# Earlier row transposes and another order of copies, scalings and key doubling in the attention of a decoder trunk

## The chip, the cores and the metric

The kernel runs on one core of a Trainium2 chip. The metric is device time in microseconds (us) of one launch. The engines are named as the profile names them: PE multiplies matrices (PEld loads its weights), DVE and ACT work on vectors and read what PE leaves in PSUM, POOL and SP issue most DMAs. Each engine works through its own queue in order, and an instruction waits at its head until what it needs is there.

## The reference

One decoder layer on 512 tokens of width 1024, in float32: two attentions side by side, merged by gates, then an MLP with a short convolution.

```python
h = _rmsnorm(x, norm1_g[l]) * (1.0 + scale1) + shift1
proj = h @ w_in[l]
qa, ka, va, qd, kd, vd, ga, gd = jnp.split(proj, points, axis=-1)
out_a = _sliding_window_attention(...)   # 8 heads, 2 key heads, window 128, sinks
out_d = _diff_attention(...)             # 4 heads, two softmax maps each, below
merged = (jax.nn.sigmoid(ga) * (out_a @ w_branch_swa[l])
          + jax.nn.sigmoid(gd) * (out_d @ w_branch_diff[l]))
x = x + gate1 * (merged @ w_out[l])
h2 = _rmsnorm(x, norm2_g[l]) * (1.0 + scale2) + shift2
x = x + gate2 * _conv_ffn(h2, ...)       # then a final rmsnorm

# inside _diff_attention, for a block of 128 queries:
p = jax.nn.softmax(scores, axis=-1)
a = p[:, :, 0] - lam * p[:, :, 1]
out = einsum('bhqs,bshe->bqhe', a, v)
# and over all blocks: each head's 128 values are normed
out = _rmsnorm(out, subln_g) * (1.0 - lam_init)
```

## The kernel before

Float32 precision is had from a faster product: every operand is split into a high part (a cast, on ACT) and a low part (the difference, on DVE), and three products high x high, high x low, low x high are summed (lines 123 to 125). So each weight tile costs PE, ACT and DVE work.

The work runs in stages: the first projections (to about 57 us of the span), the two attentions with the remaining projections between their steps (to about 250 us), the output projection, the MLP. This case is about the attentions.

**Queues.** PE's order in attention is written out by hand. `fill(n)` puts n *ticks* of projection work (three products of one 128-row piece) between the steps of attention; `after(n, fn)` calls `fn` n ticks later. DVE and ACT are ordered by a scheduler: `tc.high_priority(offset=HP)` ranks what is inside ahead of other ready work (a larger offset ranks higher), `tc.issue_after` sets a lower bound.

**Names.** `stack` (L433) makes scaled queries in two copies, one with high and low parts on swapped halves of the partitions: ACT scales the high part (L438), DVE makes the low part (L441). `qa` are the queries of the windowed attention, in four pairs of heads; pair 1 is made from `aqa1` (`acc[2]`). `qk` holds a head's queries and keys of the differential attention; `double` (L445) makes its keys: casts on ACT (L448), low parts on DVE (L450), then two copies across halves (L452), one on DVE and one on ACT. Windowed pairs: `sw` scores, `st` and `lsum` softmax, `tp` transposes on PE, `pT` their copies on ACT (L619), `oa` values. Differential heads 0 to 3, each with four query blocks n: `sd` scores (PE L675), L686 bias and minimum on DVE, L701 exponentials on ACT, L704 to L706 on DVE, `td` transposes, `aTh`/`aTl` their parts. `ta` (L787 on ACT) empties a gate's projection `pga` from one of two banks tagged "f".

**A head's norm.** `diff_values(h)` multiplies probabilities and values into `od`. ACT makes `sq` (squares) and `of` (scaled values). Six ticks later (`STAT_LAG`) PE sums the squares (`pss`, L739), DVE and POOL form the inverse root as four columns (L154 to L166). `ROW_LAG` ticks after that `to_rows` turns the columns into a row: a transpose on PE (L102), a copy on ACT (`rs0p` to `rs3p`, L105), and two DMAs on POOL's queue (L107, L108), out to DRAM and back to all partitions as `rb`. `NORM_LAG` ticks after the sums `spread` multiplies `of` by `rb` (DVE L752) and splits the product into `vvh` (ACT) and `vvl` (DVE), both by `split` (L120). `od`, `pss` and the turned row share one bank tagged "v". `ada_rows` puts 32 unrelated row sums (`ra`, L776) on DVE; `wga`, `wba`, `wgd`, `wbd` are weight tiles split on ACT and DVE; `pB` is the last product of attention that needs `vvh` and `vvl`.

Of the kernel before, what the change touches and what calls it, by code (L numbers as in the profile page):

```python
# [27 lines left out]
HP = 100000  # L28
# [2 lines left out]
ADA_EVERY = 5  # L31
G1_AT = 12
M5_AT = 4
STAT_LAG = 6
ROW_LAG = (16, 16, 16, 10)
NORM_LAG = (30, 30, 30, 24)
VA_AT = 5
SWA_FILL = (2, 1, 6, 2, 2, 2, 2, 5, 0)
# [9 lines left out]
def kernel(  # L48
# [19 lines left out]
    nc = tc.nc  # L68
# [16 lines left out]
    def fbank(name):  # L85
        return bank("f", 2, [P, S], name)

    def sbank(name, shape=(P, S)):
        return bank("s", 3, list(shape), name)
# [29 lines left out]
    def split(hi, lo, src):  # L119
        return nc.scalar.copy(hi, src), nc.vector.tensor_sub(lo, src, hi.bitcast(F32))  # L120
# [104 lines left out]
    acc = [sbank("aka"), sbank("aqa0"), sbank("aqa1"), fbank("av0"), fbank("av1"), vbank("ava"), tbank("av2"), tbank("av3")]  # L225
# [10 lines left out]
    qsc = cpool.tile([P, 4], F32, name="qsc")  # L236
# [180 lines left out]
    qa = big.tile([P, 4, 2, S], F32R, tag="qa", name="qa")  # L417
# [12 lines left out]

    halves = ((lower, upper), (upper, lower))

    def stack(dst, src, scale, soon=True, high=True, low=True):  # L433
        with tc.high_priority(offset=HP) if soon else ExitStack():
            sc = [scale if isinstance(scale, float) else scale[own] for own, _ in halves]
            for j in range(2) if high else ():
                own = halves[j][0]
                nc.scalar.activation(dst[own, j], src[own], AF.Copy, scale=sc[j])  # L438
            for j in range(2) if low else ():
                own, other = halves[j]  # L440
                nc.vector.scalar_tensor_tensor(  # L441
                    dst[other, j], src[own], sc[j], dst[own, j].bitcast(F32), ALU.mult, ALU.subtract
                )

    def double(dst, src):  # L445
        with tc.high_priority(offset=HP):
            for j, (own, _) in enumerate(halves):
                nc.scalar.copy(dst[own, j, 0], src[own])  # L448
            for j, (own, _) in enumerate(halves):
                nc.vector.tensor_sub(dst[own, j, 1], src[own], dst[own, j, 0].bitcast(F32))  # L450
            for j, (own, other) in enumerate(halves):
                (nc.vector.tensor_copy, nc.scalar.copy)[j](dst[other, j], dst[own, j])  # L452

    vv = [big.tile([P, DIFF_HEADS, S], F32R, tag=f"vv{g}", name=f"vv{g}") for g in "hl"]
    vaT = big.tile([P, S], F32, tag="sq2", name="vaT")

    def keep_v(i, parts=(0, 1)):
        t = TOKENS[i] * P
        hi, lo = (v[:, :, t : t + P] for v in vv)
        src = acc[i].rearrange("p (h d) -> p h d", d=P)  # L460
        if 0 in parts:
            nc.scalar.copy(hi, src)
        if 1 in parts:
            nc.vector.tensor_sub(lo, src, hi.bitcast(F32))
# [23 lines left out]
    nc.vector.scalar_tensor_tensor(  # L488
        qa[lower, 0, 1], acc[1][upper], qsc[upper, 0:1], qa[upper, 0, 1].bitcast(F32), ALU.mult, ALU.subtract
    )  # L490
    stack(qa[:, 1], acc[2], qsc[:, 1:2], soon=False, low=False)
    keep_v(6, (0,))
    vat_copy = nc.scalar.copy(vaT, acc[5])
    man.close()
# [51 lines left out]
    def after(n, fn):  # L546
        later.append([n, fn])
# [42 lines left out]
    def swa_softmax(i):  # L590
        with tc.high_priority(offset=HP):
            c = pairs[i]
            for j in range(2):
                h = i + 4 * j
                nc.scalar.activation(c.es[:, j], c.nm[:, j], AF.Exp, bias=sink[:, h : h + 1])
                for n in range(NT):
                    w = P if n == 0 else 2 * P
                    nc.scalar.activation(
                        c.sb[n][:, j, :w], c.sb[n][:, j, :w], AF.Exp, bias=c.nm[:, j, n : n + 1], scale=-1.0,
                        accum_out=c.lsum[:, j, n : n + 1],  # L600
                    )
                nc.vector.tensor_add(c.lsum[:, j], c.lsum[:, j], c.es[:, j])
                nc.vector.reciprocal(c.lsum[:, j], c.lsum[:, j])
                for n in range(NT):
                    w = P if n == 0 else 2 * P
                    c.end = nc.vector.tensor_scalar_mul(c.sb[n][:, j, :w], c.sb[n][:, j, :w], c.lsum[:, j, n : n + 1])

    def swa_transpose(i, j):
        c = pairs[i]
        pt = ap.tile([P, 1024], F32, tag=("aTh", "aTl")[j], bufs=2, name=f"pT{i}_{j}")  # L610
        for b in range(2):
            wb = 512 if b == 0 else 384
            tp = tbank(f"tp{i}_{j}_{b}")
            for m in range(wb // P):
                kb, n = 2 * b + m // 2, 2 * b + m // 2 + m % 2
                off = (kb - max(0, n - 1)) * P
                nc.tensor.transpose(tp[:, m * P : (m + 1) * P], c.sb[n][:, j, off : off + P], ident)
            with tc.high_priority(offset=HP):
                c.copy = nc.scalar.copy(pt[:, b * 512 : b * 512 + wb], tp[:, :wb])  # L619
        c.pT.append(pt)  # L620

# [23 lines left out]
    def add_head(h):  # L645
        def q(wts):
            t = heads[h] = ap.tile([P, 6, S], F32R, tag="qk", bufs=2, name=f"qk{h}")
            o = fbank(f"pq{h}")
            yield from steps(o, wts, hT, KT)
            stack(t[:, 0:2], o, 2.0 ** (2 * h - 1))  # L650

        def k(wts):
            t = heads[h]
            o = fbank(f"pk{h}")
            yield from steps(o, wts, hT, KT)
            double(t[:, 2:6].rearrange("p (j b) s -> p j b s", b=2), o)

        for run, n in ((q, TILE_QD), (k, TILE_KD)):
            units.append((lambda n=n: load_tile(n + h, f"w{n}_{h}"), run))
# [61 lines left out]
    def diff_values(h):  # L721
        aTh, aTl = aTs[h]
        o = vbank(f"od{h}")
        for k in range(NT):
            q0 = k * P
            mm3(
                o[:, q0:], vv[0][:, h, k * P : (k + 1) * P], vv[1][:, h, k * P : (k + 1) * P],
                aTh[:, k * AW + q0 : k * AW + 512], aTl[:, k * AW + q0 : k * AW + 512],
                k == 0, k == NT - 1,
            )  # L730
        sq = big.tile([P, S], F32, tag="sq2", name=f"sq{h}")
        of = big.tile([P, S], F32, tag=("kvA", "kvB")[h % 2], name=f"of{h}")
        nc.scalar.activation(sq, o, AF.Square)
        nc.scalar.activation(of, o, AF.Copy, scale=sublnc)

        def stats():
            pss = vbank(f"pss{h}", (P, NT))
            for n in range(NT):
                nc.tensor.matmul(pss[:, n : n + 1], sq[:, n * P : (n + 1) * P], ones[:, 0:1], start=True, stop=True)  # L739
            rs = cols[:, NCOL + NT * h : NCOL + NT * h + NT]  # L740
            l0, e0 = sums[h][:, 0], sums[h][:, 1]
            nc.vector.scalar_tensor_tensor(e0, l0, EPS, l0, ALU.mult, ALU.mult)
            with tc.high_priority(offset=HP):
                rstd_m2(rs, pss, NT, P, ap, plus=e0)
            last = h == DIFF_HEADS - 1
            rb = big.tile([P, S], F32, tag="sq2", name="rb3") if last else ap.tile([P, S], F32, tag="rb", name=f"rb{h}")

            def spread():
                with ExitStack() as place:
                    for b in recent:  # L750
                        place.enter_context(tc.issue_after(b.ins))
                    nc.vector.tensor_mul(of, of, rb)  # L752
                split(vv[0][:, h], vv[1][:, h], of)

            after(ROW_LAG[h], lambda: to_rows(rb, NCOL + NT * h, NT, f"rs{h}"))
            after(NORM_LAG[h], spread)

        after(STAT_LAG, stats)


    def ada_behind(op):
# [60 lines left out]
    with tc.issue_after(pairs[0].last.ins), tc.issue_after(vat_copy.ins):  # L822
        with tc.high_priority(offset=HP):
            keep_v(6, (1,))
            keep_v(4, (1,))
        swa_softmax(0)
        stack(qa[:, 1], acc[2], qsc[:, 1:2], soon=False, high=False)
        keep_v(7, (1,))

        lp = cpool.tile([P, 2, 64], F32, tag="part", name="lp")  # L830
        ls = cpool.tile([P, 2], F32, name="ls")
        nlam = cpool.tile([P, 1], F32, name="nlam")
        nc.vector.tensor_mul(lp, lamv[:, 0:4:2], lamv[:, 1:4:2])
        nc.vector.reduce_sum(ls, lp, axis=mybir.AxisListType.X)
        nc.scalar.activation(ls, ls, AF.Exp)
        nc.vector.tensor_sub(nlam, ls[:, 1:2], ls[:, 0:1])
        nc.vector.tensor_scalar_add(nlam, nlam, -LAM_INIT)
        fill(VA_AT)
        turn_va()
        fill(SWA_FILL[2] - VA_AT)  # L840
# [30 lines left out]
    for s in range(4 * DIFF_HEADS):  # L871
        h, n = divmod(s, NT)
# [981 lines left out]
```

## Time and profile before

| | |
|---|---|
| time, median of 3 runs | 686.05 us (685.69 to 687.92) |
| time of the profiled execution | 685.63 us |
| its span, first to last instruction | 683.9 us |
| PE busy | 668.9 us, 98% |
| DVE busy | 567.4 us, 83% |
| ACT busy | 397.4 us, 58% |
| mean granted PE clock | 0.996 |

In rows of waits: the engine that waited and its line, the engine and line that ended it, us in total, times, longest. In rows of the timeline and the chain: start and length in us, engine, line, operation, output<-input. A bracket gives the idle time before an instruction and what ended it. Times are counted from the start of the span.

### The profile page before, as it was taken

What the parts mean: (1) busy time and instruction counts of PE and PEld (TensorE: products, weight loads), DVE (VectorE), ACT (ScalarE), POOL (GpSimd) and SP (SyncE); (2) the same over time, 40 slices, a digit from 0 to 9 for tenths busy, and PEclk for the clock granted to TensorE, in tenths of its full rate; (3) what the DMA queues carried; (4) which work ended last, traced back from release to release, by engine and by line L of the source; (5) the groups of instructions that cost most, each with busy time, mean ns of one, the idle gap of its engine ahead of it and who ended that gap; (6) DMA issues with size and microseconds to landing.
All of it is one profiled execution on the core that took longest, in us unless ns stands there. A gap on an engine that the chain in (4) does not pass through costs nothing.

```text
span 683.9 us, 10773 instructions
## 1 busy us (share of the span) xinstructions
PE 668.9 (98%) x4021; PEld 592.5 (87%) x4021; DVE 567.4 (83%) x1023; ACT 397.4 (58%) x700; POOL 73.4 (11%) x86
## 2 busy tenths in 40 slices
PE   8999999999999999999999999999999999999995
PEld 7888878888778878888899999999999998888885
DVE  6987997779767668974689998888888999979997
ACT  6678777465543323333488565666555666656665
POOL 2000000010001100010020110111111003540300
PEclk9999999999999999999999999999999999999999
DMA  8961231454345488758572989787867657996903
GB/s 351 409 237 61 88 99 62 131 152 150 108 139 176 154 281 286 270 128 305 155 124 85 224 217 209 183 194 187 203 166 187 153 181 187 197 200 192 168 0 124
DMA packets 71876, 121.78 MB, mean 178 GB/s; under 512 B 4208, under 2 KB 48016, under 8 KB 71824
## 3 DMA queue, kind: packets, MB, share of 16 engines
q1 hardware_dynamic: 52960, 95.04, 41.5%
q0 software_dynamic: 18576, 25.71, 22.3%
q8 instruction: 31, 0.51, 0.3%
q10 hardware_dynamic: 288, 0.34, 0.2%
q14 instruction: 21, 0.17, 0.1%
HBM read 118.97 MB, written 2.11 MB: 177 GB/s over the span
## 4 chain that ended last, share of the span: by engine, by line
PE 85%; DVE 6%; DMA 4%; ACT 3%; issue 2%; DVEq 0%; ACTq 0%; POOLq 0%
PE up L1180 32%; PE dc L1783 15%; PE av L366 3%; PE oc L1237 2%; PE oc L1240 2%; PE oc L1236 2%; PE aqa L363 2%; PE pgd L125 2%; PE pgd L123 2%; PE pgd L124 2%; PE pga L123 1%; PE pga L124 1%; PE pga L125 1%; DMA ra<-in_w_ada_t_dram 1%; PE sd L675 1%
## 5 line engine op out<-in xcount | busy, mean ns | idle before, releaser
L1180 PE MATMUL up<-t,m_whi 128*128 128x256 f32 x512 | 93.1, 283 | 0.0
L1180 PEld LDWEIGHTS up<-t,m_whi 128*128 128x128 f32 x512 | 79.9, 192 | 0.0
L1180 PE MATMUL up<-t,m_wlo 128*128 128x256 f32 x256 | 72.4, 283 | 0.0
L1180 PE MATMUL up<-bh,p_whi 128*128 128x256 f32 x232 | 65.7, 283 | 0.0
L1180 PE MATMUL up<-bl,p_whi 128*128 128x256 f32 x232 | 65.7, 283 | 0.0
L1180 PE MATMUL up<-bh,p_wlo 128*128 128x256 f32 x232 | 65.7, 283 | 0.0
L1180 PEld LDWEIGHTS up<-t,m_wlo 128*128 128x128 f32 x256 | 49.2, 192 | 0.0
L1180 PEld LDWEIGHTS up<-bh,p_whi 128*128 128x128 f32 x232 | 44.5, 192 | 0.0
L1180 PEld LDWEIGHTS up<-bl,p_whi 128*128 128x128 f32 x232 | 44.5, 192 | 0.0
L1180 PEld LDWEIGHTS up<-bh,p_wlo 128*128 128x128 f32 x232 | 44.5, 192 | 0.0
L1082 POOL DMA_DIRECT2D s<-in_w_up_dram x21 | 27.0, 1366 | 157.7 <-DMA s<-in_w_up_dram 102.2
L776 DVE CUSTOM_DVE_ANT_0 ra<-ra,csb 128x1024 f32<-128x1024 f32 x32 | 38.6, 1219 | 3.7 <-DMA ra<-in_w_ada_t_dram 3.6
L1110 ACT CAST m_whi<-s 128x1024 fp32r<-128x1024 f32 x31 | 32.5, 1048 | 15.7 <-DVE s L1104 9.1
L1114 DVE TENSOR_TENSOR m_wlo<-s,m_whi 128x1024 fp32r<-128x1024 f32 x31 | 37.7, 1217 | 1.3 <-ACT m_whi L1110 1.3
L1180 PE MATMUL up<-t,p_whi 128*128 128x256 f32 x176 | 32.2, 283 | 0.0
L701 ACT ACTIVATE sd<-sd,dmx 128x128 f32<-128x128 f32 (+3 forms) x32 | 17.7, 554 | 17.3 <-DVE dmx L686 17.2
L1180 PEld LDWEIGHTS up<-t,p_whi 128*128 128x128 f32 x176 | 27.4, 192 | 0.1
L1110 ACT CAST p_whi<-wa 128x1024 fp32r<-128x1024 f32 x18 | 18.8, 1043 | 12.6 <-PE up L1180 5.4
L1187 ACT ACTIVATE gT<-a,cols 128x512 f32<-128x512 f32 x22 | 17.6, 813 | 13.4 <-DVE a L1222 13.0
L1114 DVE TENSOR_TENSOR p_wlo<-wa,p_whi 128x1024 fp32r<-128x1024 f32 x18 | 22.0, 1221 | 4.0 <-ACT p_whi L1110 3.3
L1180 PE MATMUL up<-t,p_wlo 128*128 128x256 f32 x88 | 24.9, 283 | 0.0
L1104 DVE TENSOR_TENSOR s<-s,wa 128x1024 f32<-128x1024 f32 x20 | 24.3, 1217 | 0.1
(546 smaller groups left out, 2030.6 us busy)
## 6 DMA issues: line engine op xcount, KB each, us to landing
ra<-in_w_ada_t_dram SPq DMA_DIRECT2D x32, 512.0 KB, 3.9
wa<-in_w_up_dram SPq DMA_DIRECT2D x22, 512.0 KB, 4.5
s<-in_w_up_dram SPq DMA_DIRECT2D x21, 512.0 KB, 4.6
s<-in_w_up_dram POOLq DMA_DIRECT2D x21, 512.0 KB, 6.7
adaw<-in_w_ada_t_dram SPq DMA_DIRECT2D x15, 512.0 KB, 10.2
a<-in_w_up_dram SPq DMA_DIRECT2D x11, 512.0 KB, 4.8
b<-in_w_down_dram SPq DMA_DIRECT2D x10, 512.0 KB, 4.4
w<-in_w_first_dram SPq DMA_DIRECT2D x8, 512.0 KB, 10.2
```

The source lines that it names most:

```text
L123: nc.tensor.matmul(o, lh, rh, start=start, stop=False)
L124: nc.tensor.matmul(o, lh, rl, start=False, stop=False)
L125: nc.tensor.matmul(o, ll, rh, start=False, stop=stop)
L366: nc.tensor.matmul(acc[i], ht[:, t : t + P], wts[k][w][:, S:], start=start, stop=stop)
L701: nc.scalar.activation(pm[m], pm[m], AF.Exp, bias=mx[:, m : m + 1], scale=-1.0, accum_out=(l0, l1)[m])
L776: nc.vector.tensor_tensor_reduce(r, r, csb, 1.0, 0.0, ALU.mult, ALU.add, late_mod[:, idx : idx + 1])
L1082: nc.gpsimd.dma_start(dst, upblock(*blk), accum_op=ALU.add)
L1104: nc.vector.tensor_add(src, src, R[J, "a11" if name == "m6" else "a12"])
L1110: nc.scalar.copy(W[J, name][0], R[J, SRC[name]])
L1114: nc.vector.tensor_sub(lo, R[J, SRC[name]], hi.bitcast(F32))
L1180: nc.tensor.matmul(o[u], w[:, k, cu], b[:, k], start=name in ("p1", "m5", "p2") and k == 0 and x == 0, stop=k == 3 and x == 2, skip_group_ ...
L1783: nc.tensor.matmul((bank2[u] if o is None else o)[:, sl], a[:, q, cu], b[:, q, sl], start=first_mm and x == 0, stop=last_mm and x == 2, sk ...
```

## The change

Five edits; the number of products, of tiles and of DMAs stays the same. The row transposes of the four heads come 8, 8, 8 and 5 ticks behind the sums. The low parts of the second pair's queries are ranked high and written ahead of the first softmax. `pT` copies get twice the rank. The queries and keys of heads 0 and 1 get half of it. For heads 2 and 3 both copies of doubled keys run on ACT. The split of `of * rb` into `vvh` and `vvl` gets a rank.

```diff
-STAT_LAG = 6
-ROW_LAG = (16, 16, 16, 10)
+STAT_LAG = (6, 6, 6, 6)
+ROW_LAG = (8, 8, 8, 5)
...
-    def stack(dst, src, scale, soon=True, high=True, low=True):
-        with tc.high_priority(offset=HP) if soon else ExitStack():
+    def stack(dst, src, scale, soon=HP, high=True, low=True):
+        with tc.high_priority(offset=soon) if soon else ExitStack():
...
-    def double(dst, src):
-        with tc.high_priority(offset=HP):
+    def double(dst, src, soon):
+        with tc.high_priority(offset=soon):
...
-                (nc.vector.tensor_copy, nc.scalar.copy)[j](dst[other, j], dst[own, j])
+                (nc.scalar.copy if j or soon == HP else nc.vector.tensor_copy)(dst[other, j], dst[own, j])
...
-    stack(qa[:, 1], acc[2], qsc[:, 1:2], soon=False, low=False)
+    stack(qa[:, 1], acc[2], qsc[:, 1:2], soon=0, low=False)
...
-            with tc.high_priority(offset=HP):
+            with tc.high_priority(offset=2 * HP):
                 c.copy = nc.scalar.copy(pt[:, b * 512 : b * 512 + wb], tp[:, :wb])
...
-            stack(t[:, 0:2], o, 2.0 ** (2 * h - 1))
+            stack(t[:, 0:2], o, 2.0 ** (2 * h - 1), HP if h > 1 else HP // 2)
...
-            double(t[:, 2:6].rearrange("p (j b) s -> p j b s", b=2), o)
+            double(t[:, 2:6].rearrange("p (j b) s -> p j b s", b=2), o, HP if h > 1 else HP // 2)
...
-                split(vv[0][:, h], vv[1][:, h], of)
+                with tc.high_priority(offset=HP):
+                    split(vv[0][:, h], vv[1][:, h], of)
...
-        after(STAT_LAG, stats)
+        after(STAT_LAG[h], stats)
...
+        stack(qa[:, 1], acc[2], qsc[:, 1:2], high=False)
         swa_softmax(0)
-        stack(qa[:, 1], acc[2], qsc[:, 1:2], soon=False, high=False)
```

Three places of the resulting orders. Rows name the line, the operation and output<-input; lines behind 753 of the changed kernel are one higher. First ACT's queue around the row copy of head 1, `rs1p`, while heads 2 (`wga`, `td_0`) and 3 (`qk_1704`, scores `sd_0_0` to `sd_1_1`) go on. Before:

```order
L701 ACTIVATE sd_3_1_1867,dls_1709<-sd_3_1_1867,dmx_3_1864 128x512
L120 CAST wba_h<-wba_1969 128x1024
L787 ACTIVATE ta<-pga_1854 128x512
L701 ACTIVATE sd_0_0_1915,dls_1945<-sd_0_0_1915,dmx_0_1914 128x128
L701 ACTIVATE sd_1_0_1920,dls_1945<-sd_1_0_1920,dmx_1_1919 128x256
L701 ACTIVATE sd_0_1_1917,dls_1945<-sd_0_1_1917,dmx_0_1914 128x128
L701 ACTIVATE sd_1_1_1922,dls_1945<-sd_1_1_1922,dmx_1_1919 128x256
L424 CAST aTh_1748<-td_3_1938 128x4x128
L120 CAST wga_h<-wga_1976 128x1024
L105 COPY rs1p<-rs_1989 32x128
```

After:

```order
L448 CAST qk_1704<-pk_1784 64x512 x2
L452 COPY qk_1704<-qk_1704 64x1024 x2
L701 ACTIVATE sd_3_0_1865,dls_1716<-sd_3_0_1865,dmx_3_1864 128x512
L424 CAST aTh_1748<-td_2_1884 128x3x128
L701 ACTIVATE sd_3_1_1867,dls_1716<-sd_3_1_1867,dmx_3_1864 128x512
L105 COPY rs1p<-rs_1901 32x128
L120 CAST wba_h<-wba_1976 128x1024
```

`rs1p` moves from behind the next head's exponentials to right behind `sd_3_1`; ahead of it both key copies (L452) are now ACT's.

Second, ACT's queue between the gate `ta<-pga_2078` and the row's use at head 2; `sq_2218` and `of_2219` are head 3's, `vvh<-of_2028` head 2's. Before:

```order
L787 ACTIVATE ta<-pga_2078 128x512
L120 CAST wga_h<-wga_2179 128x1024
L424 CAST aTh_2005<-td_3_2159 128x4x128
L105 COPY rs2p<-rs_2195 32x128
L733 ACTIVATE sq_2218<-od_2205 128x512
L734 ACTIVATE of_2219<-od_2205,cols 128x512
L120 CAST wgd_h<-wgd_2333 128x1024
L787 ACTIVATE ta<-pga_2185 128x512
L120 CAST vvh<-of_2028 128x512
```

After:

```order
L788 ACTIVATE ta<-pga_2078 128x512
L105 COPY rs2p<-rs_2145 32x128
L120 CAST wga_h<-wga_2186 128x1024
L424 CAST aTh_2005<-td_3_2166 128x4x128
L120 CAST vvh<-of_2028 128x512
L733 ACTIVATE sq_2218<-od_2205 128x512
L734 ACTIVATE of_2219<-od_2205,cols 128x512
L120 CAST wgd_h<-wgd_2333 128x1024
L788 ACTIVATE ta<-pga_2192 128x512
```

`rs2p` goes two places ahead, `vvh` four, past head 3's `sq` and `of`.

Third, DVE's queue at the last head's low part (`vvl<-of_2219`). Before:

```order
L752 TENSOR_TENSOR of_2219<-of_2219,rb_2256 128x512
L120 TENSOR_TENSOR wgd_l<-wgd_2447,wgd_h 128x1024
L776 ISA ra_2463,late_mod<-ra_2463,csb 128x1024
L776 ISA late_mod 128x1
L776 ISA ra_2482,late_mod<-ra_2482,csb 128x1024
L776 ISA late_mod 128x1
L120 TENSOR_TENSOR vvl<-of_2219,vvh 128x512
```

After:

```order
L752 TENSOR_TENSOR of_2219<-of_2219,rb_2256 128x512
L120 TENSOR_TENSOR wgd_l<-wgd_2447,wgd_h 128x1024
L120 TENSOR_TENSOR vvl<-of_2219,vvh 128x512
L777 ISA ra_2463,late_mod<-ra_2463,csb 128x1024
L777 ISA late_mod 128x1
```

`vvl` passes the two row sums.

## The prediction

> **What bounds the kernel now.** The page first, then the waits of PE, the granted clock in windows around the worst of them, and the chain back from there.
>
> ```profile
> span 683.9 us, 10773 instructions
> PE 668.9 (98%) x4021; PEld 592.5 (87%) x4021; DVE 567.4 (83%) x1023; ACT 397.4 (58%) x700; POOL 73.4 (11%) x86
> ```
>
> PE is the bound: the edits add no matrix product and take none away, so they can only return time in which PE stands still, or runs slowly. The waits of PE:
>
> ```profile
> PE pB L124 <- DVE vvl L120: 1.7, 1, 1.7
> PE tp L617 <- ACT pT L619: 1.3, 2, 0.9
> PE pga L123 <- ACT ta L787: 1.2, 1, 1.2
> ...
> PE sw L579 <- DVE qa L441: 0.6, 1, 0.6
> PE sd L675 <- DVE qk L452: 0.5, 1, 0.5
> ...
> PE sd L675 <- DVE dmx L686: 0.3, 1, 0.3
> ```
>
> These six come to 5.6 us, all between 67 and 250 us, in attention; after that PE has no wait worth a row. Windows around the third (columns: length, busy us of PE, PEld, DVE, ACT, POOL, granted clock, DMA share, GB/s) show a second loss:
>
> ```profile
> 199.89:203.30 3.41, 2.24 (x15) 1.96 (x14) 1.47 (x3) 1.43 (x3) 0.00 (x0) 1.00 0.39 104
> 203.30:206.71 3.41, 3.41 (x10) 2.65 (x10) 2.96 (x9) 2.09 (x6) 0.91 (x1) 0.51 0.12 20
> ...
> 247.66:251.07 3.41, 1.73 (x8) 1.13 (x7) 3.27 (x6) 2.10 (x3) 0.16 (x1) 1.00 0.82 241
> ```
>
> Behind the stall at 202 the clock is granted at 0.51 for 3.41 us, which costs 0.49 x 3.41 = 1.67 us more. So 5.6 + 1.7 = 7.3 us is the most that can be had. What stands behind the 202 stall is in the chain of work, in order of time:
>
> ```profile
> 191.32 0.27 ACT rs1p L105
> ...
> 196.09 5.04 DMA rb<-rs1d
> 201.15 0.70 DVE of L752
> 201.87 0.62 ACT vvh L120
> 202.49 0.50 ACT ta L787
> ```
>
> A row of roots makes a trip through DRAM. DVE has reached `of` (L752) before it lands and stands; ACT stands behind it at `vvh`, which is queued ahead of `ta`; PE wants the bank that `ta` empties. The waits of DVE show the same at every head:
>
> ```profile
> DVE of L752 <- DMA rb<-rs2d: 6.7, 1, 6.7
> DVE of L752 <- DMA rb<-rs1d: 5.4, 1, 5.4
> ...
> DVE of L752 <- DMA rb<-rs3d: 3.8, 1, 3.8
> ...
> DVE of L752 <- DMA rb<-rs0d: 2.2, 1, 2.2
> ```
>
> **The change part by part.** Times are of this profiled execution (685.63 us, of which 683.9 is span); the median of the three runs is 0.42 above it.
>
> *Second queries first, copies of pT first.* In the low parts of the second queries the change moves two DVE operations ahead of the softmax sums; PE's scores that waited 0.6 us for them find them ready. DVE's work stays the same in kind and number. The pT copy that PE waited 0.9 us for (the longer of two waits, 1.3 in all, so the other is 0.4) stood on ACT behind two `qk` scalings:
>
> ```profile
> 85.12 1.20 ACT L438 ACTIVATE qk<-pq 64x512 fp32r<-64x512 f32 x2
> 86.34 0.97 ACT L619 COPY pT<-tp 128x512 f32<-128x512 f32 x2
> ...
> 98.54 0.51 ACT L598 ACTIVATE st<-st,nm 128x256 f32<-128x256 f32 x1
> 99.17 0.97 ACT L619 COPY pT<-tp 128x512 f32<-128x512 f32 x2
> ```
>
> The scalings of 1.2 us now go behind it, which covers 0.9. But I credit little of the 1.5, because DVE is the second bound here:
>
> ```profile
> 85.00:90.00 5.00, 4.05 (x26) 3.31 (x25) 4.91 (x13) 4.49 (x13) 0.00 (x0) 1.00 0.48 163
> ```
>
> 4.91 of 5 us busy: what PE no longer waits, DVE does not make up. Walked through in the new order, DVE gains about 0.5 in the first of these waits (it stood idle there for sums of ACT), ends pair 2's query parts 0.15 after PE asks for them, and reaches pair 3's scores at its old time, while PE is then 1.4 sooner. The next pT copy (99.17) stands behind four exponentials, at 0.5 or less each, where it stood behind two of them and two casts of keys: 0.6 sooner. So PE's wait there grows from 0.4 by 1.4 - 0.6 = 0.8. Net of this part: 0.6 + 0.9 - 0.15 - 0.8 = 0.55 us won; bounds 0 (DVE holds all of it back) and 1.9 (0.6 + 1.3, all kept). The lower rank of the `qk` work of heads 0 and 1 costs nothing more: their first scores come more than 10 us behind it, with PE's projections between; without that cover it would cost the 1.2 us of a pair of scalings.
>
> *Doubled keys of heads 2 and 3 on ACT.* DVE's copy goes, ACT makes both:
>
> ```profile
> 183.25 1.04 ACT L452 CAST qk<-qk 64x1024 fp32r<-64x1024 f32 x1 [2.98 <-DVE qk L450]
> 184.03 0.41 PE L675 MATMUL sd<-qk 128*128 128x128 f32 x2 [0.50 <-DVE qk L452]
> 185.55 0.71 ACT L701 ACTIVATE sd<-sd,dmx 128x512 f32<-128x512 f32 x1
> ```
>
> In series on ACT they take 2.08 us; before, the other ran beside this one on DVE. Head 2's lie some 3 us ahead of their scores: free. Head 3's are what PE waited 0.5 and 0.3 for, from 183.5 on. Row 0 now lands before DVE asks for it (it stood 2.2 us), but in the next 8 us DVE comes to sums that PE has not yet made and to a power on POOL, and arrives at the low parts of the keys only 0.7 sooner. ACT's first copy then starts near 181.85 and its second ends 2.1 later, near 183.95, for scores that want the first at 183.5 and the second a quarter of a us later: a wait of 0.3. The 0.5 so won is lost again at the next transposes (a wait of 0.2 before), since ACT still ends the exponentials for them at 185.55 + 0.71 = 186.26. Net 0.1; bounds -0.9 (one copy more, nearly in full) and 1.0 (both waits and the 0.2 behind).
>
> *Rows of roots sooner.* PE turns each row 8 (head 3: 5) ticks behind the sums instead of 16 (10). POOL and SP keep their orders: a row's two DMAs are issued on POOL ahead of the next head's power, as before, and are over before that is asked for. `STAT_LAG` becomes a table of equal numbers, which moves nothing. For head 1, ACT's `rs1p` moves from 191.32 to right behind the exponential that ended at 186.26: 5.1 sooner against a wait of 5.4, so `of` starts near 201.15 - 5.1 = 196.05. Behind it come `vvh` (0.62), `sq` and `of` of head 2 (0.60 and 0.68, rows below), a cast of weights (1.05) and `ta` (0.60): 196.05 + 0.70 + 3.55 = 200.3, where PE wanted the bank 1.17 before 203.04, at 201.87. Won: 1.17 + 1.67 = **2.84 us**. Bounds 1.17 (the clock falls for another reason) and 2.84.
>
> The clock fell here behind a window with 2.24 us busy, about 0.95 of that the one-column products of `pss` (a row below has such a group); it did not fall behind the later window with 1.73, all of it wide products. [...]
>
> For head 2 the gain is smaller, and there is a new queue:
>
> ```profile
> 203.13 0.55 DVE L686 CUSTOM_DVE_ANT_0 sd<-sd,ddf 128x384 f32<-128x384 f32 x1
> 213.05 0.60 ACT L787 ACTIVATE ta<-pga 128x512 f32<-128x512 f32 x1
> 217.34 0.26 ACT L105 COPY rs2p<-rs 32x128 f32<-32x128 f32 x1 [1.36 <-issue]
> 220.28 0.60 ACT L733 ACTIVATE sq<-od 128x512 f32<-128x512 f32 x1 [2.69 <-PE od L125]
> 220.77 0.68 ACT L734 ACTIVATE of<-od,cols 128x512 f32<-128x512 f32 x1
> 222.84 1.05 ACT L120 CAST wgd_h<-wgd 128x1024 fp32r<-128x1024 f32 x1 [1.38 <-issue]
> 224.18 0.94 PE L739 MATMUL pss<-ones,sq 128*128 128x1 f32 x8
> 226.03 0.69 DVE L752 TENSOR_TENSOR of<-of,rb 128x512 f32<-128x512 f32 x1 [6.67 <-DMA rb<-rs2d]
> ```
>
> `rs2p` now stands behind `ta`, which ended at 213.65. DVE begins this stretch (203.13) 2.2 sooner, since `wga_l` is put first and must await its cast, so `rs2p` falls near 211.4; PE runs 2.84 sooner. The trip took 226.03 - 217.34 = 8.7, so `of` starts near 220.1. On ACT `vvh` now stands *ahead* of `sq` and `of` of head 3: 0.69 + 0.62 + 0.6 + 0.68 with handovers is 2.6, done at 222.7. PE's sums `pss` want them (and their bank) at 224.18 - 2.84 = 221.3: a new stall of **1.4 us**, with the next products of PE queued behind it. Behind it ACT still has `wgd_h` (1.05), DVE its low part and then the root, ready near 227.1; PE turns row 3 five ticks behind the sums, at 227.0: 0.2. Bounds: none (the row in time) and 4.6 (below).
>
> *Low part of the last head first.*
>
> ```profile
> 245.17 0.69 DVE L752 TENSOR_TENSOR of<-of,rb 128x512 f32<-128x512 f32 x1 [3.75 <-DMA rb<-rs3d]
> 245.78 1.22 DVE L120 TENSOR_TENSOR wgd_l<-wgd,wgd_h 128x1024 fp32r<-128x1024 f32 x1
> ...
> 249.20 0.68 DVE L120 TENSOR_TENSOR vvl<-of,vvh 128x512 fp32r<-128x512 f32 x1
> ```
>
> `vvl` goes ahead of the two `ra` rows, to 247.0, and row 3 comes sooner too. It ends before 247.7; PE came to it at 248.3. Won **1.7**; the rows behind it are not on PE's path here.
>
> Sum: 0.55 + 0.1 + 2.84 - 1.6 + 1.7 = **3.6 us**, call it 3.5: 682.1 on the profiled execution, **682.5** on the median. What follows (256 us on) is PE without waits, so the shift is kept.
>
> **The rivals.** A measurement of this kernel can tell 0.3%, 2.06 us, from no change: faster means under 684.0, slower over 688.1.
>
> - *Row 2 in time* (chance 0.15): the row lands 1.5 us sooner than I have it, and head 2 costs nothing. For it: DMA was idle in parts of that stretch. 3.5 + 1.6 = 5.1: 680.9; with all early waits kept too, 679.8.
> - *The clock falls at head 2* (0.20): my 1.4 us stall joins the 0.95 us of one-column `pss`, and 2.35 us of little work is what preceded the fall at 203 (1.17 + 0.95 = 2.1). [...] 3.5 - 1.7 = 1.8: 684.3.
> - *The half-clock stretch is not the stall's* (0.05): it stays somewhere, and 1.17 is won of 2.84. 3.5 - 1.67 = 1.8: 684.2. [...]
> - *The rows do not come sooner* (0.07): ACT's copies keep their places behind other work, and only `vvl` (1.7) counts. 684.4.
> - *Slower* (0.08): ACT at head 2 is blocked by the row. If its trip takes what row 3's took, 245.17 - 233.52 (its copy, below) = 11.65 instead of 8.7, the stall is 1.4 + 2.95 = 4.35 and with `pss` covers more than a window; two windows at half clock cost 3.3. -3.5 + 2.95 + 3.3 = +2.75: 688.8. It decides from a trip of about 10.5 us on, with one such window (-3.5 + 1.8 + 1.7 = 0).
>
> ```profile
> 233.52 0.26 ACT L105 COPY rs3p<-rs 32x128 f32<-32x128 f32 x1
> ```
>
> **How the numbers follow.** Forecast 0.45. Faster: nearly all of the forecast (0.42), the first rival (0.15), and the lower parts of those at 684.2 to 684.4 (0.10): 0.67. Slower 0.08, the rest 0.25. The range reaches from 679.8 to 685.6 (the clock rival with nothing kept of the early part and of `qk`, 684.3 + 0.65, and 0.65 for a less favourable trip); outside lie the slower rival and tails.
>
> **What would show it.** Right: the waits of DVE for `rb` of rows 0, 1 and 3 gone, that of row 2 near 3 us; PE's waits for `ta` and `vvl` gone; the window behind 203 at full clock; a new PE wait at `pss` for ACT's `sq` or `of` near 220, and one near 99 for pT about 1 us. Wrong: a half-clock stretch elsewhere in attention, a PE wait for row 3's `cols` over 1 us, or waits of PE for scores near 116 or 184 that grow because ACT now makes both key copies.

## The result

The changed kernel took **683.37 us** (median of 20 runs, 681.54 to 685.95) against 686.22 for the kernel before (20 runs beside it, 685.23 to 688.87): ratio 0.9961, 95% interval 0.9949 to 0.9973, or 2.7 us (1.9 to 3.5) won. The forecast was 682.5, in a range of 679.8 to 685.6. The profiled execution took 684.42 us.

The profile after. Its page, and the waits of PE between 55 us and the end:

```profile
span 682.6 us, 10775 instructions
PE 668.4 (98%) x4021; PEld 592.6 (87%) x4021; DVE 566.5 (83%) x1021; ACT 399.7 (59%) x702; POOL 72.8 (11%) x86
PE pss L739 <- ACT of L734: 2.6, 1, 2.6
PE tp L617 <- ACT pT L619: 0.8, 1, 0.8
PE od L124 <- DVE aTl L425: 0.6, 1, 0.6
PE pga L125 <- DVE wga_l L120: 0.6, 1, 0.6
PE td L716 <- DVE sd L706: 0.5, 1, 0.5
```

Of the six waits of before, `vvl` (1.7), `ta` (1.2), `qa`, `qk` and `dmx` are gone, and `tp` fell from 1.3 to 0.8. A seventh, `td`, grew from 0.2 to 0.5, and `od` and `wga_l` are new. So the sum of all of them fell from 5.8 to 5.1 us only, since `pss` alone waits 2.6. Of DVE's four waits for rows one is left, 5.1 us for row 2, where the forecast said near 3; it stands in the timeline below.

The granted clock in windows (columns as before) behind the old stall near 202 us, and around the new one at 220.5:

```profile
203.14:206.55 3.41, 3.41 (x18) 2.77 (x17) 3.07 (x10) 0.05 (x1) 0.31 (x1) 1.00 0.09 35
...
220.21:223.63 3.42, 0.78 (x6) 0.47 (x5) 1.38 (x2) 2.21 (x4) 0.00 (x0) 1.00 0.06 24
223.63:227.04 3.41, 3.41 (x13) 2.83 (x13) 1.67 (x5) 1.85 (x3) 1.04 (x1) 0.54 0.21 53
```

The half-clock stretch behind 203 us is gone, and one stands behind 223.6. The timeline there (POOL's row is the issue of the DMA that spreads the row):

```profile
209.84 0.26 ACT L105 COPY rs2p<-rs 32x128 f32<-32x128 f32 x1
214.97 0.57 POOL L108 DMA_DIRECT2D rb<-rs2d  x1 [4.00 <-DMA rs2d<-rs2p]
220.70 0.69 DVE L752 TENSOR_TENSOR of<-of,rb 128x512 f32<-128x512 f32 x1 [5.15 <-DMA rb<-rs2d]
221.42 0.62 ACT L120 CAST vvh<-of 128x512 fp32r<-128x512 f32 x1 [9.57 <-DVE of L752]
221.94 0.59 ACT L733 ACTIVATE sq<-od 128x512 f32<-128x512 f32 x1
222.43 0.68 ACT L734 ACTIVATE of<-od,cols 128x512 f32<-128x512 f32 x1
223.16 1.21 PE L739 MATMUL pss<-ones,sq 128*128 128x1 f32 x8 [2.64 <-ACT of L734]
```

This is the forecast's new stall, in its place and by its queue: the row is late, `vvh` waits for it on ACT, and head 3's `sq` and `of` wait behind `vvh`, ready to run since PE ended `od` at 216.4. It is 2.6 us long and not 1.4. The row's trip took 220.70 - 209.84 = 10.86 us and not 8.7, but its copy came 1.6 us sooner than forecast (209.84, not 211.4), so `of` started only 0.6 late (220.70, not 220.1). And PE came to the sums at 223.16 - 2.64 = 220.52, 0.8 sooner than the 221.3 of the forecast. Of the trip the spreading DMA (KB, median us from issue to landing) took 5.7 us. Its row, and the window from its issue to `of`; then the same of the kernel before:

```profile
rb<-rs2d POOLq DMA_DIRECT2D x1, 256.0 KB, 5.7
214.97:220.70 5.73, 5.56 (x28) 4.44 (x27) 0.58 (x3) 0.00 (x0) 0.57 (x1) 1.00 0.74 237
...
rb<-rs2d POOLq DMA_DIRECT2D x1, 256.0 KB, 3.8
222.17:226.03 3.86, 3.86 (x23) 3.32 (x22) 0.00 (x1) 1.54 (x2) 0.57 (x1) 1.00 0.41 118
```

Sent earlier, it flew while the DMA engines were busy at 0.74 (237 GB/s); before, at 0.41 (118 GB/s).

### The profile page after: what moved, and what is told of

Read it like the earlier page. It is cut to its first block, busy times and chain, and to the rows that moved or that the text cites. A ratio compares the mean times of both kernels' runs of the same rounds, so it can differ in the third digit from the quotient of the medians.

```text
span 682.6 us, 10775 instructions
## 1 busy us (share of the span) xinstructions
PE 668.4 (98%) x4021; PEld 592.6 (87%) x4021; DVE 566.5 (83%) x1021; ACT 399.7 (59%) x702; POOL 72.8 (11%) x86
## 4 chain that ended last, share of the span: by engine, by line
PE 66%; DVE 1%; ACT 0%; issue 0%; ACTq 0%
PE up L1181 33%; PE dc L1784 15%; PE pgd L123 2%; PE oc L1241 2%; PE pgd L124 2%; PE oc L1237 2%; PE oc L1238 2%; PE pgd L125 2%; PE pB L124 1%; PE pB L123 1%; PE pB L125 1%; PE th L1277 1%; PE pga L123 0%; PE pA L123 0%; PE pga L125 0%; PE pga L124 0%
## 5 line engine op out<-in xcount | busy, mean ns | idle before, releaser
L156 POOL TENSOR_TENSOR r<-ms,mhalf 128x4 f32<-128x4 f32 x4 | 5.1, 1266 | 181.7 <-DVE ms L154 181.7
```

## The experiments

Each was timed in five rounds beside the kernel before on the same chip; a gain in us is the ratio's. The recorded expectations count by medians instead (2.85 for the whole change, 1.5 for the key copies).

**Head 2's row four ticks later.** The stall taken away by itself. (Four ticks are twelve products on PE; the "three products" of the expectation are a slip.)

```diff
-ROW_LAG = (8, 8, 8, 5)
+ROW_LAG = (8, 8, 12, 5)
```

> The changed kernel with the lag of head 2's row of roots at 12 in place of 8: the row's product comes three products later on TensorE, and ScalarE has head 2's high part `vvh` behind head 3's `sq` and `of` again; nothing else moves. Theory (the stall of 2.6 us before `pss3` is the queue on ScalarE, and the half-clock window behind it is its child): the wait for `pss` falls below 0.3 us, the window behind 223 us runs at full clock, and the median comes 2.6 to 4.3 us below the changed kernel's 683.4, at 679.1 to 680.8. Rival 1 (the window isn't the stall's): only the 2.6 us, 680.8, and the clock still falls near 223. Rival 2 (the time is given back, because `vvh` and `vvl` of head 2 are then late for the products of the last stage): 683 to 684, with a wait for `vvh` or `vvl` near 240 us.

680.87 us; ratio 0.9932 (0.992 to 0.9944): 4.7 us below before, 2.0 better than the changed kernel. PE's waits from 120 us on, and the place of the stall:

```profile
PE pga L123 <- ACT ta L788: 0.7, 1, 0.7
...
PE rs L102 <- DVE cols L166: 0.4, 1, 0.4
...
215.86 0.60 ACT L733 ACTIVATE sq<-od 128x512 f32<-128x512 f32 x1 [3.98 <-PE od L125]
219.75 0.95 PE L739 MATMUL pss<-ones,sq 128*128 128x1 f32 x8
220.07 0.69 DVE L752 TENSOR_TENSOR of<-of,rb 128x512 f32<-128x512 f32 x1 [5.13 <-DMA rb<-rs2d]
```

`of` still starts at 220.1, but `sq` no longer stands behind the row, and the mean granted clock is 0.998, where the changed kernel's is 0.994. So the queue on ACT made the stall. The gain falls short of the 2.6 to 4.3 expected: two small waits (`ta`, `cols`, together 1.1) come up in its place.

**The rows alone.** The kernel before, one line changed.

```diff
-ROW_LAG = (16, 16, 16, 10)
+ROW_LAG = (8, 8, 8, 5)
```

> The kernel before with the new lags of the rows (8, 8, 8, 5) and nothing else. Theory (steps read from the two traces): 2.9 us won at head 1 (stall for `ta` and the half-clock window behind it), 2.6 us lost at the new stall before `pss3`, 1.7 us more where the clock falls there, about 2.0 us won at the last `vvl`: 0.6 to 2.3 us below before's 686.2, 683.9 to 685.6. Rival (the rows are the whole of the change, the other edits nothing): 683.4. Rival (the new stall eats it all): 686.2.

684.73 us; ratio 0.999 (0.9979 to 1.0002): 0.7 us, inside the theory's span. PE's waits and the window behind 224.9 show why it is so little:

```profile
PE pss L739 <- ACT of L734: 2.6, 1, 2.6
...
PE od L124 <- DVE aTl L425: 0.8, 1, 0.8
PE pga L123 <- ACT ta L787: 0.7, 1, 0.7
...
224.90:228.30 3.40, 3.40 (x10) 2.63 (x10) 2.11 (x6) 1.23 (x2) 1.04 (x1) 0.57 0.39 119
```

The stall at `pss` and its half-clock window come with the rows, and give back most of what heads 1 and 3 win; the wait for `ta` is not gone either. The queue order is the rows' doing too: with the plain rank for the value split, `vvh` of head 2 stands ahead of `sq` here as well.

**The row of head 1 alone.**

```diff
-ROW_LAG = (16, 16, 16, 10)
+ROW_LAG = (16, 8, 16, 10)
```

> The kernel before with the row of head 1 at lag 8 and the three others as they were. It prices head 1's row alone. Term on record: 2.84 us (1.17 stall and 1.67 window). From the landmarks of the run with all four rows early: 2.9 us at 217 us, of which head 0's row had 0.6; so 2.3 us, 683.3, with the wait for `ta` at 0.7 us or less, no half-clock window near 203 us, and the wait for `vvl` near 248 us as before, 1.7 to 1.9. Rival (VectorE's piece of work after the row keeps its end near 217 us): nothing gained, 685.6.

683.1 us; ratio 0.9962 (0.995 to 0.9973): 2.6 us. This one number is worth as much as the whole change. PE's waits:

```profile
PE od L124 <- DVE aTl L425: 0.9, 1, 0.9
...
PE pga L123 <- ACT ta L787: 0.2, 1, 0.2
```

The wait for `ta` fell from 1.2 to 0.2, and a new one, for `aTl` of head 3, is in the list. The granted clock is 1.00 in every half microsecond of attention. The waits for `vvl` (1.7 to 1.1) and for `qk` (0.5 to 1.1) moved too, one each way.

**The stall for `ta` filled with work.** Is the half-clock window behind it worth 1.67 us?

```diff
-            pss = vbank(f"pss{h}", (P, NT))
+            pss = vbank(f"pss{h}", (P, NT + P))
...
+            for _ in range(8 if h == 2 else 0):
+                nc.tensor.matmul(pss[:, NT:], ones, ones, start=True, stop=True)
...
-                rstd_m2(rs, pss, NT, P, ap, plus=e0)
+                rstd_m2(rs, pss[:, :NT], NT, P, ap, plus=e0)
```

> The kernel before with eight more products (ones times ones, 128x128, unused columns of the bank of `pss2`) behind the sums of head 2, about 1.1 us of work in the 1.17 us that TensorE waits for `ta`; nothing else changes. Theory on record: the half-clock window behind 203 us goes, and the time falls by 1.67 us. Theory now (behind the window TensorE runs into a wait for `aTl` near 216 us, since VectorE has 16 us of work in one piece from the row's arrival on): the window goes, the wait for `aTl` grows from nothing to 1.2 us, and the time stays within 0.3 us of before. Rival (the window isn't the stall's): the window stays, the time the same.

686.13 us; ratio 1.0008 (0.9995 to 1.0021): nothing won. The profiled execution, at 684.62, is the fastest of the eleven; the others reach to 688.43. The fillers, the window behind them, and PE's wait:

```profile
201.46 2.03 PE L741 MATMUL pss<-ones 128*128 128x128 f32 x16
203.25 0.48 PE L123 MATMUL pga<-hThA,wga_h 128*128 128x512 f32 x1
...
203.22:206.63 3.41, 3.41 (x19) 2.81 (x18) 3.37 (x8) 1.44 (x5) 0.00 (x0) 1.00 0.34 124
...
PE od L124 <- DVE aTl L425: 1.0, 1, 1.0
```

The fillers took 203.25 - 201.46 = 1.79 us, some 0.6 more than the stall, so with the window worth 1.67 the time should still have fallen by 1.0; the interval excludes that. The window is gone and PE meets a wait of 1.0 for `aTl` instead. In the kernel before, DVE sets that point:

```profile
203.13:218.22 15.09, 15.06 (x63) 11.84 (x63) 13.01 (x33) 7.38 (x16) 1.73 (x2) 0.89 0.39 116
...
217.54 0.68 DVE L425 TENSOR_TENSOR aTl<-td,aTh 128x512 fp32r<-128x512 f32 x1
218.28 0.50 PE L124 MATMUL od<-aTl,vvh 128*128 128x512 f32 x1
```

From head 1's row on DVE is busy for 13.0 of 15.1 us, and its `aTl` ends at 218.22, just when PE comes to it, slowed by the half clock. With the window filled PE takes the same product at 217.85, 0.4 sooner and not 1.0, again as soon as `aTl` is there. So the window cost little or nothing: it lay beside DVE's work. What made the slower executions of this run slow is not shown; they have no trace.

**Second queries, scalings and pT copies alone.** The changed kernel with the rows' lags, the key copies and the split's rank of before.

```diff
-ROW_LAG = (8, 8, 8, 5)
+ROW_LAG = (16, 16, 16, 10)
...
-                (nc.scalar.copy if j or soon == HP else nc.vector.tensor_copy)(dst[other, j], dst[own, j])
+                (nc.scalar.copy if j else nc.vector.tensor_copy)(dst[other, j], dst[own, j])
...
-                with tc.high_priority(offset=HP):
-                    split(vv[0][:, h], vv[1][:, h], of)
+                split(vv[0][:, h], vv[1][:, h], of)
```

> The changed kernel with the rows' lags, the keys' copies and the plain rank of the value split of before: only the second queries, the scalings and the copies of transposed probabilities keep their new ranks. Theory (the head start of 0.45 us that the traces show from 124 to 178 us stays to the end): 0.45 us below before, 685.8. Rival 1 (all 1.5 us that the changed kernel is ahead at 193 us are these edits'): 684.7. Rival 2 (the head start is swallowed by the stall at head 1, which a row's transfers time): 686.2.

685.19 us; ratio 0.9995 (0.9986 to 1.0003): 0.3 us, near the 0.55 on record; no gain is not excluded, the rival of 1.5 is. PE's waits:

```profile
PE pB L124 <- DVE vvl L120: 1.9, 1, 1.9
PE pga L123 <- ACT ta L787: 1.2, 1, 1.2
PE od L124 <- DVE aTl L425: 1.2, 1, 1.2
...
PE pga L125 <- DVE wga_l L120: 0.6, 1, 0.6
```

In this execution the clock stayed at 1.00 from 199.73 to 206.55 although the wait for `ta` is as long as ever, and PE waits 1.2 for `aTl`: the same exchange as with the fillers. (The next run, of the key copies, fits it: a wait of 1.1 for `ta`, 1.2 for `aTl`, and a mean granted clock of 0.998, where before has 0.996.) The wait for `wga_l` near 116 us is a price that the forecast did not have.

**The key copies alone.** The kernel before, both copies of heads 2 and 3 on ACT.

```diff
-                (nc.vector.tensor_copy, nc.scalar.copy)[j](dst[other, j], dst[own, j])
+                (nc.scalar.copy if j or both else nc.vector.tensor_copy)(dst[other, j], dst[own, j])
...
-            double(t[:, 2:6].rearrange("p (j b) s -> p j b s", b=2), o)
+            double(t[:, 2:6].rearrange("p (j b) s -> p j b s", b=2), o, h > 1)
```

> The kernel before with both key copies of heads 2 and 3 on ScalarE and nothing else. Theory on record: 0.1 us won, 686.1. Rival (the two traces' landmarks move apart by 1.1 us between 178 and 193 us, where head 3's keys are doubled): 1.1 us won, 685.1. Rival (ScalarE's copies hold its exponentials back): slower by up to 0.9 us, 687.1.

684.08 us; ratio 0.9985 (0.9975 to 0.9995): 1.0 us, not 0.1. Head 3's keys, from DVE's low parts to PE's scores:

```profile
180.34 1.40 DVE L450 TENSOR_TENSOR qk<-pk,qk 64x512 fp32r<-64x512 f32 x2
181.05 2.12 ACT L452 CAST qk<-qk 64x1024 fp32r<-64x1024 f32 x2 [1.74 <-DVE qk L450]
183.27 1.08 PE L675 MATMUL sd<-qk 128*128 128x128 f32 x8
```

In the kernel before, these low parts began at 181.76. Now DVE comes to them 1.4 us sooner, ACT has both copies done at 183.17, and the scores do not wait. The lead on DVE comes from row 0. Its use before, and in this run:

```profile
173.91 0.69 DVE L752 TENSOR_TENSOR of<-of,rb 128x512 f32<-128x512 f32 x1 [2.20 <-DMA rb<-rs0d]
...
171.66 0.69 DVE L752 TENSOR_TENSOR of<-of,rb 128x512 f32<-128x512 f32 x1
```

ACT's copy of this row starts at 165.33 before and at 165.24 here, but the trip takes 6.4 us and not 8.6, and DVE no longer waits for it. Nothing of the row was edited; why it came sooner was not tested.

**The key copies back in the changed kernel.**

```diff
-                (nc.scalar.copy if j or soon == HP else nc.vector.tensor_copy)(dst[other, j], dst[own, j])
+                (nc.scalar.copy if j else nc.vector.tensor_copy)(dst[other, j], dst[own, j])
```

> The changed kernel with the key copies of heads 2 and 3 as before (one on VectorE, one on ScalarE), all else changed. The keys alone took 1.5 us off the kernel before. Theory 1 (the parts add up: 0.4 + 1.5 + 0.9 is the whole 2.85): the keys are worth 1.5 here too, and the time stands 1.3 us below before. Theory 2 (rows and keys relieve the same queue on VectorE near 184 to 190 us, where the rows alone gained 0.6 to 1.2 us too): the keys are worth 0.4 here, 2.4 us below before. Theory on record (0.1): 2.75 us below before.

684.35 us; ratio 0.9978 (0.9966 to 0.9991): 1.5 us below before, so the copies are worth about 1.2 in the changed kernel. Theory 1 (1.3) is nearest; the interval, 0.6 to 2.3, all but reaches theory 2 (2.4). Its waits show another place than with the copies alone: the early rows already spare the scores their wait, and without ACT's copies `ta` and `aTl` wait longer.

```profile
PE od L124 <- DVE aTl L425: 0.9, 1, 0.9
PE pga L123 <- ACT ta L788: 0.6, 1, 0.6
```

**The stall at `pss` filled, first try.** Fillers in the bank of `pss3`, as above, in the changed kernel: `range(18 if h == 3 else 0)`, ahead of the sums.

> The changed kernel with eighteen such products ahead of the sums of head 3, about 2.4 us of work in the 2.6 us that TensorE waits for `of`; ScalarE and VectorE keep their order. Theory: the stall's length stays, but TensorE is busy in it, so no half-clock window follows; no wait stands behind to take the gain back (none from 224 us to the end), so runs with a window at head 3 lose it, 1.7 us each: the median falls from 683.4 to about 681.8, 4.4 us below before, and all runs stand close together. Rival (the clock doesn't go by how busy TensorE is): the window near 224 us stays, 2.85 us below before.

686.53 us; ratio 1.0014 (1.0005 to 1.0024). It filled nothing:

```profile
221.91 5.91 PE L739 MATMUL pss<-ones 128*128 128x128 f32 x36 [2.26 <-ACT of L734]
...
222.98:226.40 3.42, 3.42 (x18) 3.42 (x18) 1.07 (x1) 1.24 (x2) 0.00 (x0) 0.50 0.38 125
```

The first filler itself waits for `of`: the bank was `od`'s, which `of` reads. So the wait at `pss` is for the bank as well as for the squares. The fillers came on top of it, and the half-clock window came as before, now over the fillers.

**Second try, in a free bank.**

```diff
+            if h == 3:
+                spare = sbank("spare", (P, P))
+                for _ in range(18):
+                    nc.tensor.matmul(spare, ones, ones, start=True, stop=True)
             pss = vbank(f"pss{h}", (P, NT))
```

> The changed kernel with eighteen products of ones ahead of the sums of head 3, this time in a bank of the scores, which is free there; in the first try they stood in the bank of `pss3`, waited for `of` themselves, and filled nothing. About 2.4 us of work in the 2.6 us that TensorE waits for `of`; the other engines keep their order. Theory: the wait for `pss` shrinks below 0.4 us, no half-clock window follows it, and the granted clock of most runs is 0.996 or more: 1.7 us off most runs, the median near 681.7, 4.4 us below before. Rival (the window comes by something else): it stays near 224 us, 2.85 us below before.

683.26 us; ratio 0.9967 (0.9955 to 0.9978): as the changed kernel, where 681.7 was expected. The window behind the stall, and PE from the fillers to row 3's transpose:

```profile
223.63:227.04 3.41, 3.41 (x24) 3.05 (x23) 1.77 (x6) 1.35 (x2) 1.04 (x1) 1.00 0.36 106
...
220.14 4.18 PE L740 MATMUL spare<-ones 128*128 128x128 f32 x36
224.16 0.95 PE L743 MATMUL pss<-ones,sq 128*128 128x1 f32 x8
228.52 0.27 PE L102 MATMUL rs<-ident,cols 128*128 128x128 f32 x1
...
221.93 0.68 ACT L734 ACTIVATE of<-od,cols 128x512 f32<-128x512 f32 x1
```

Half clock is gone, and the six executions have mean granted clocks of 0.996 to 0.998, where 17 of the changed kernel's 20 have 0.992 to 0.995. From `pss` to the transpose PE needs 228.52 - 224.16 = 4.36 us; in the changed kernel it needed 6.03:

```profile
229.19 0.27 PE L102 MATMUL rs<-ident,cols 128*128 128x128 f32 x1
```

So here the window costs its full 1.67 us, and it does follow from the standstill: from 220.21 to 223.63 PE was busy for 0.78 of 3.42 us in the changed kernel and for all 3.42 here. But each filler takes 0.22 us, not the 0.13 I had reckoned with, which is near the 1.08 us of eight score products (L675) of that shape: eighteen took 4.0 us, and ACT had finished `of` at 222.61, 1.5 before them. The fillers ate what they gave. The mechanism is shown, the gain in time is not.

**Towards a better version.** Head 2's row at 12, and the splits of `outa` at the lowest rank, so that `wga_l` goes ahead of them on DVE:

```diff
-        evac(outa[0][:, i], outa[1][:, i], o)
+        with tc.high_priority(offset=-HP):
+            evac(outa[0][:, i], outa[1][:, i], o)
```

> The changed kernel with head 2's row at lag 12 (as in the run of the first set that was 4.7 us below before) and the splits of the window attention's outputs at the lowest rank: VectorE then has `wga_l` ahead of the first `outal`, behind which TensorE waited 0.6 us near 116 us and lost 0.9 us of its head start. Theory: 0.6 to 0.9 us better than that run, 5.3 to 5.6 us below before. Rival (VectorE has as much to do before 124 us as ever, and the later splits hold back head 0's softmax): no gain, 4.7 us below before.

679.52 us; ratio 0.9914 (0.99 to 0.9927): 5.9 below before, a little more than the 5.3 to 5.6 expected, and the wait for `wga_l` is gone. Then also `ROW_LAG = (8, 8, 12, 7)`:

> As the version with head 2's row at lag 12 and the late splits of `outa` (6.0 us below before), and head 3's row at lag 7 in place of 5, so that TensorE no longer waits 0.38 us for row 3's `cols` near 224 us. Theory: 0.4 us better, 6.4 below before. Rival (row 3 then lands some 3 us later, and `vvl` of the last head, done 2 us before TensorE wants it, is late by 1 us): 0.6 worse, 5.4 below before.

678.92 us; ratio 0.9902 (0.9889 to 0.9916): **6.7 us below before**, 4.0 better than the changed kernel, the fastest version run. All of PE's waits worth a row from 55 us on:

```profile
PE tp L617 <- ACT pT L619: 0.9, 1, 0.9
PE td L717 <- DVE sd L707: 0.5, 1, 0.5
```

## Why the prediction was right, and where its steps were not

The sign and size came out, 0.9 us from the forecast, but partly by luck: errors in the parts cancel.

- *Second queries and pT* (0.55): 0.3 measured, within 1.0 and -0.2. DVE was the second bound, as argued; the wait near 99 us grew, from 0.3 to 0.8, less than the forecast's 0.4 to 1.2. What it lacked is the next place where PE meets DVE: near 116 us PE came sooner, but `wga_l` ended no sooner on DVE (116.15, and 116.05 before), since a split of `outa` now stood ahead of it, and PE waited 0.6.
- *Key copies* (0.1, bounds -0.9 and 1.0): 1.0 alone. The term was mis-sized in "arrives at the low parts of the keys only 0.7 sooner": it is 1.4 in the run of the copies alone, 1.6 with the rows alone (180.19 for 181.76) and 1.8 in the changed kernel (179.96). In all three DVE takes head 0's `of` at 171.3 to 171.7 without a wait, against 173.91 before. So the lead is row 0's, and the early rows have it without the copies.
- *Head 1's row* (2.84 = 1.17 + 1.67): 2.6 measured alone, but not by that sum. The stall term held; the window term of 1.67 failed. The step that failed is the unwritten one behind it, that PE keeps what it wins at full clock. DVE's `aTl` sets where they meet next: PE starts the product that needs it 0.05 to 0.06 us behind its end at 218.28 before, 217.85 with the fillers, 217.56 with the early edits, 216.99 with the key copies and 216.71 with this row, and only the first of these had the window. The row is worth 2.6 because it moves DVE's piece of work too, 1.6 us at this point; its trace shows the wait for `vvl` shorter by 0.6 besides. I had named DVE as second bound near 85 us and not looked for it here.
- *Head 2's row* (-1.6): the mechanism as forecast, mis-sized. Trip 10.86 for 8.7, stall 2.64 for 1.4, and the half-clock window on top, 1.67, which was also one of the signs named for being wrong. That is the rival "the clock falls at head 2", to which I gave 0.20; its 684.3 is nearest to the profiled execution's 684.42. The trip was taken from before, from a stretch with DMA at 0.41; moved earlier it met one at 0.74. The rival "slower" put its turning point at a trip of 10.5 with one such window; both came and the change still won, since the copy was 1.6 sooner than forecast and other parts gave more. Its two windows at half clock were an estimate from the 1.67 of one; behind the stall of 2.64 one came. The expected 0.2 at row 3's `cols` is not in the list.
- *`vvl`* (1.7): PE's wait is gone, and was 1.0 to 1.9 in every run with row 3 at its old place. It is gone with the rows alone too, where `vvl` still stands behind the `ra` rows but the stall at `pss` made PE later; the rank of the split was not run by itself.
- *The granted clock*: ahead of the fall PE was busy for 0.78 of 3.42 us here, and for 2.24 of 3.41 ahead of the fall of before. With the early edits alone it was busy for 2.22 of 3.41 up to 203.14, and the clock stayed at 1.00. So the busy time of the stretch ahead does not settle it; what does, no run shows.

Measured apart, rows 0.7, key copies 1.0 and early edits 0.3 come to 2.0, and together 2.7; within the intervals they add up. Why the copies keep their worth in the changed kernel, where neither the scores nor row 0 make anyone wait, stays open; their absence shows there as longer waits for `ta` and `aTl`.

## What to carry to other kernels

A lost stretch on the bound engine is worth only as far as the second engine's queue is ahead of it (the 1.67 us behind the stall for `ta` were worth nothing to the fillers): follow that engine to the next place where the two meet before counting stall or clock. A transfer's duration belongs to the stretch in which it ran (head 2's spread took 3.8 us before, 5.7 after); moved, it must be priced anew. And an instruction that waits for a transfer must not be queued ahead of ready work whose bank or result the bound engine wants: four ticks of delay there were worth 2 us.

## What the runs showed of the hardware

- The same half-clock window, 3.41 us long, is close to free in one place and costs its full 1.67 us in another (the fillers at `ta`, against 4.36 and 6.03 us at `pss`). The executions without a trace fit, as far as a mean clock tells: it is a rough sign, 0.996 both in the profiled execution of before, with a window, and in that of the spare bank, without one. Of 67 runs of the kernel before beside the experiments, the 18 with a mean granted clock up to 0.995 had a median of 685.58 us, the 49 above it 685.54. Of the changed kernel's 20, those at 0.996 to 0.997 had 681.8 (3 runs), at 0.994 to 0.995 683.3 (10), at 0.992 685.3 (7): steps of 1.5 and 2.0, which would fit a window each, and its trace has no wait of PE behind 224 us that could absorb one.
- A float32 product of 128x128 by 128x128 took 0.22 us and stands as two records in the trace. Of the products of split parts, 128x128 by 128x512, PE starts one every 0.23 us in the changed kernel (at 217.19, 217.42, 217.65).
- A spread of 256 KB from one row took from 3.7 to 5.8 us at head 2 in the 13 traces. Over all four heads of the kernels before and after it took 3.4 to 4.1 us with the DMA engines busy at 0.35 to 0.62 in its time, and 5.0 to 7.1 at 0.66 to 0.95; the share alone does not settle it (5.0 at 0.86, 5.7 at 0.74), and no run varied it by itself.
